# A hybrid attention and RWKV-7 block on one core: the recurrence cut into six parts a step for both directions side by side, and the first norm of the later tokens computed once and kept in DRAM

## The chip, the cores and the metric

The kernel runs on one core of one Trainium2 chip. TensorE (PE) does the matrix products, VectorE (DVE), ScalarE (ACT) and GpSimd (POOL) the element work, SyncE (SP) starts the transfers. The metric is the device time of one execution in microseconds (us).

## The reference, cut to what matters

One layer of a hybrid block over 2048 latent tokens and 256 context tokens, width 1024. What matters here is the first half of the layer, from the first norm to the merge of the two branches; the MLP behind it is the same in both kernels.

```python
h = modulate(rmsnorm(x, norm1_g), shift1, scale1)
hc = modulate(rmsnorm(xc, norm1_g), modc[0], modc[1])
q, k, v, rw, gl = jnp.split(h @ w_in, IN_SPLITS, axis=-1)
qc, kc, vc, rwc, glc = jnp.split(hc @ w_in, IN_SPLITS, axis=-1)
...
ya = latent_window_attention(q, k, v, kc, vc, sink)      # 16 blocks of 128 queries
...
for d, rev in enumerate((False, True)):                  # the recurrence, one scan a direction
    S_ctx, yc_d = wkv7_scan(S0, r_c, dec_c, kk_c, b_c, k_c, v_c, rev, update_ctx)
    _, y_d = wkv7_scan(S_ctx, r_l, dec_l, kk_l, b_l, k_l, v_l, rev, True)
    y_lat.append(y_d)
yr = rwkv_output(y_lat[0] + y_lat[1], r_l, v_l, hg_l, dirs_l, gate_g2, r_k, lnx_w, lnx_b)

x = x + gate1 * merge_branches(ya, yr, gl, w_branch_attn, w_branch_rwkv, w_out)
x = x + gate2 * sq_relu_mlp(modulate(rmsnorm(x, norm2_g), shift2, scale2), w_mlp_up, w_mlp_down)
```

## The kernel before, in words

The kernel has four stages. Each float32 product with weights is made of three matmuls on operands split in a high and a low part (`hh` and `hl` for the tokens, `w_hi` and `w_lo` for the weights).

**Stage 1** (0 to some 1060 us) is the first norm and the projection by `w_in`. The tokens are taken in three passes (`THIRDS`: 256 and 512, then 384 and 512, then 384 and 256 tokens), and each pass runs over 20 groups of weight columns. Ahead of each pass, `norm_block` loads the tokens of its two blocks, norms them (`x`, L180), transposes them on PE (`tr`, L186), scales (`hf`, L188, DVE) and splits them (`hh` on ACT, L192, `hl` on POOL, L193). `h_d` keeps `hf` for the first 1024 latent tokens, whose merge gates are computed later. Behind each pass `prepare` computes the inputs of the recurrence for those 256-token windows that are ready.

**Stage 2** (to 2540 us) is the recurrence with other work beside it. Per direction there are 36 steps of 64 tokens (`NCH`, `C`). For each window of four steps, `gram` makes small products (`g`, L517), and `inverse` inverts the 64x64 triangles on DVE: two long transposes of `ga` (`au`, L528), 31 small pairs of `itmp` (L534) and `tn` (L536), two long transposes into `st` (L545), and then two products on PE (`yp` L557, `zp` L569) with a third DVE transpose `t` (L549) ahead of them. This runs one window ahead. Each step of a direction has a `before` (its loads, `tb` and `gb`: L606 and L613) and a `chain`: products into one PSUM tile (`ch0` or `ch1`), a copy to `g` (L626, DVE), the product by `st` (L629), two copies into `w` (L630 ACT, L631 DVE), the next state (L636, L639, `w` L642) and the output (L650, L654). Beside every second step the function `beside` adds one whole attention block (`sc` scores, `mm` their minima, `sT` and `ops` the outputs), three columns of merge gates (`gt`, L215 to L217), and pieces of the second modulation (`adp`, L117 with `ada_w`); the last windows add four products of the attention branch (`branch`, `gt` L881 to L883, input `ya_h`, L873).

**Stage 3** (to 2900 us) is the merge, which begins with transposes of `yT` (`mt`, L990), and **stage 4** the MLP.

A scheduler orders the instructions of each engine when the kernel is built, by its own simulation of time; on the chip each engine then runs its list in that order. The pools of stage 2 get their memory when those of stage 1 are closed.

Of the kernel before, what the change touches and what calls it, by code (L numbers as in the profile page):

```python
# [47 lines left out]
def tile_hybrid_block(ctx: ExitStack, tc: tile.TileContext, io: dict, out: bass.AP):  # L48
# [8 lines left out]
    h_d = dram.tile([P, KC, GL8R], F32, name="h_d")  # L57
# [114 lines left out]
    def norm_block(t0, n, tag):  # L172
        hi = hpool.tile([P, KC, n], F32R, name=f"hh_{t0}", tag=f"hh{tag}")
        lo = hpool.tile([P, KC, n], F32R, name=f"hl_{t0}", tag=f"hl{tag}")
# [8 lines left out]
        for k in range(KC):  # L183
# [279 lines left out]
    def norms(blocks):  # L463
        return [norm_block(t0, n, "a" if i == 0 else "b") for i, (t0, n) in enumerate(blocks)]

    hs = norms(THIRDS[0])
    for i, wins in enumerate(ready):
        project(THIRDS[i], hs, groups[:20])
# [20 lines left out]
    atp = p2.enter_context(tc.tile_pool(name="atp", bufs=2, space=PSUM, reuse_waits="tile"))  # L489
    WS = 4  # L490
# [15 lines left out]
    def gram(ga, step, d):  # L506

        c = order[d][step]
        u0 = place(step, d)
        ka = rp.tile([P, NP, C], F32, name="kg")  # L510
        sp.dma_start(out=ka, in_=ka_d[d, c])
        bk = rp.tile([P, NP, P], F32, name="bkg")
        sp.dma_start(out=bk, in_=bk_d[d, c])
        g = bank(auxp, "g", "aux").rearrange("p (a b) -> p a b", b=C)
        for p in range(NP):
            for r in hh:
                pe.matmul(g[r, p], bk[r, p, 0:C], ka[r, p], start=True, stop=True)  # L517
        act.activation(ga[:, u0:u0 + NP], g[:, 0:NP], AF.Copy)

    def inverse(gl, sts):  # L520
# [10 lines left out]
        for k in range(31, 0, -1):  # L531
# [5 lines left out]
            if k % 6 == 0:  # L537
                yield
# [14 lines left out]
        for u0 in range(0, NU, HU):  # L553
            yp = bank(auxp, "yp", "aux").rearrange("p (u t) -> p u t", u=HU)
            for u in range(HU):
                for h in range(2):
                    pe.matmul(yp[h * C + 32:h * C + C, u], gl[h * C:h * C + 32, u0 + u, 32:64],  # L557
# [6 lines left out]
        for u0 in range(0, NU, HU):  # L564
            zp = bank(auxp, "zp", "aux").rearrange("p (u t) -> p u t", u=HU)
            for u in range(HU):
                for h in range(2):
                    r = slice(h * C + 32, h * C + C)
                    pe.matmul(zp[h * C:h * C + 32, u], ys[r, u0 + u], st[r, u0 + u, 32:64], start=True, stop=True,  # L569
# [9 lines left out]
    def open_step(step, d):  # L579
        s = Step()  # L580
        s.step, s.d, s.c, s.u = step, d, order[d][step], place(step, d)

        s.w = rp.tile([P, 2, 2, NP, C], F32, name="w", bufs=3)
        return s

    def before(s):

        d, c = s.d, s.c

        s.kr = rp.tile([P, 3, NP, C], F32, name="kr", bufs=3)  # L590
        bk = rp.tile([P, NP, 2, C], F32, name="bks")
# [11 lines left out]
        bk = bk.rearrange("p a b t -> p a (b t)")  # L603
        tb = bank(auxp, "tb", "aux").rearrange("p (a b) -> p a b", a=NP)
        for p in range(NP):
            pe.transpose(tb[:, p], bk[:, p], ident)  # L606
        s.bt = rp.tile([P, NP, P], F32, name="bt", bufs=3)
        act.activation(s.bt, tb, AF.Copy)
        s.bm = rp.tile([P, 2, NP, C], F32, name="bm", bufs=3)
        gs = [bank(auxp, "gb", "aux").rearrange("p (a j t) -> p a j t", j=2, a=NP) for h in range(2)]  # L610
        for p in range(NP):
            for h, r in enumerate(hh):
                pe.matmul(gs[h][:, p], bk[r, p], s.kr[r, h:3:2 - h, p], start=True, stop=True)  # L613
        for h in range(2):
            q = hh[1 - h]
            dve.tensor_tensor(out=s.kr[q, h], in0=gs[h][q, :, 0], in1=strict[q], op=ALU.mult)
            dve.tensor_tensor(out=s.bm[:, h], in0=gs[h][:, :, 1], in1=incl, op=ALU.mult)

    def chain(st, s, nxt):
        d, c, w = s.d, s.c, s.w  # L620
        cp = chp.tile([P, 2, NP, C], F32, name=f"ch{d}")
        for p in range(NP):
            for h, r in enumerate(hh):
                pe.matmul(cp[r, 0, p], s.kr[:, h, p], w[:, 1, h, p], start=True, stop=True)
        g = rp.tile([P, NP, C], F32, name="g")
        dve.tensor_copy(g, cp[:, 0])  # L626
        for p in range(NP):
            for r in hh:
                pe.matmul(cp[r, 0, p], st[r, s.u + p], g[r, p], start=True, stop=True)  # L629
        act.activation(w[0:C, 0, 0], cp[0:C, 0], AF.Copy)  # L630
        dve.tensor_copy(w[C:P, 0, 1], cp[C:P, 0])  # L631
        last = None
        if nxt is not None:

            for h, r in enumerate(hh):
                pe.matmul(cp[r, 0], ident[r, r], w[r, 1, h], start=True, stop=False, skip_group_check=True)  # L636
            for p in range(NP):
                for h, r in enumerate(hh):
                    last = pe.matmul(cp[r, 0, p], s.bt[:, p, r], w[:, 0, h, p], start=False, stop=True,  # L639
                                     skip_group_check=True)  # L640
            for h, r in enumerate(hh):
                dve.tensor_tensor(out=nxt.w[r, 1, h], in0=cp[r, 0],  # L642
                                  in1=pc[r, d, :, c:c + 1].broadcast_to([C, NP, C]), op=ALU.mult)
        if s.step < NCC:
            return
        yp = cp[:, 1]
        with tc.issue_after(last.ins) if last is not None else ExitStack():
            for p in range(NP):
                for h, r in enumerate(hh):
                    pe.matmul(yp[r, p], w[:, 0, h, p], s.bm[:, h, p], start=(p == 0), stop=False,  # L650
                              skip_group_check=True)
            for p in range(NP):
                for h, r in enumerate(hh):
                    pe.matmul(yp[r, p], w[r, 1, h, p], s.kr[r, 2, p], start=False, stop=True, skip_group_check=True)  # L654
        i = s.step - NCC
        lc = c - NCC
        src = yp if d == 0 else yp[:, :, ::-1]
        ysb = rp.tile([P, NP, C], F32, name="ysb")
# [671 lines left out]
```

## Time and profile before

| | us |
|---|---|
| median of 3 runs | 4351.41 |
| lowest and highest | 4349.32 and 4365.3 |
| profiled execution, its own time | 4355.38 |
| its span in the trace | 4353.6 |
| PE busy | 3976.6 (91%) |
| DVE, ACT, POOL busy | 2233.9, 1305.1, 1344.6 |

The span is the time from the first to the last instruction of the profiled execution; its own time lies 1.78 us above it, and 3.97 us above the median. The mean granted clock of PE was 0.929 of full speed. PE is busy nearly all the time, but its list also waits at certain places; the prediction reads the trace stage by stage for that.

### The profile page before, as it was taken

What the parts mean: (1) busy time and instruction counts of PE and PEld (TensorE: products, weight loads), DVE (VectorE), ACT (ScalarE), POOL (GpSimd) and SP (SyncE); (2) the same over time, 40 slices, a digit from 0 to 9 for tenths busy, and PEclk for the clock granted to TensorE, in tenths of its full rate; (3) what the DMA queues carried; (4) which work ended last, traced back from release to release, by engine and by line L of the source; (5) the groups of instructions that cost most, each with busy time, mean ns of one, the idle gap of its engine ahead of it and who ended that gap; (6) DMA issues with size and microseconds to landing.
All of it is one profiled execution on the core that took longest, in us unless ns stands there. A gap on an engine that the chain in (4) does not pass through costs nothing.

```text
span 4353.6 us, 67896 instructions
## 1 busy us (share of the span) xinstructions
PE 3976.6 (91%) x26788; PEld 3218.5 (74%) x26788; DVE 2233.9 (51%) x3918; ACT 1305.1 (30%) x2332; POOL 1344.6 (31%) x1120
## 2 busy tenths in 40 slices
PE   7989969894899999989989768998999999999999
PEld 5868868793677777767767646777888888888887
DVE  2264286687556646656674245434444436443434
ACT  3353444553322322223222213332222123212121
POOL 3353554542111111001000046523433233433332
PEclk8979989895999999889989779999999999999999
DMA  6555556665444543354453145452211113221111
GB/s 216 143 183 155 160 159 190 175 200 177 140 116 123 165 128 112 112 144 147 120 160 110 45 133 186 161 172 75 83 54 58 39 55 120 73 63 50 48 49 49
DMA packets 581874, 527.84 MB, mean 121 GB/s; under 512 B 118452, under 2 KB 492948, under 8 KB 580532
## 3 DMA queue, kind: packets, MB, share of 16 engines
q1 hardware_dynamic: 581556, 523.50, 39.9%
q8 instruction: 211, 3.46, 0.3%
q14 instruction: 107, 0.88, 0.1%
HBM read 383.19 MB, written 140.18 MB: 120 GB/s over the span
## 4 chain that ended last, share of the span: by engine, by line
PE 59%; DVE 9%; DMA 4%; issue 2%; POOL 2%; ACT 1%; SPq 1%; POOLq 0%; DVEq 0%; ACTq 0%
PE fd L1185 5%; PE fd L1184 5%; PE fd L1186 5%; PE fu L215 5%; PE fu L216 5%; PE fu L217 5%; PE gb L613 2%; PE ops L788 2%; DVE st L545 1%; PE sc L744 1%; DVE itmp L534 1%; PE mm L1099 1%; PE mm L1100 1%; PE mm L1101 1%; DVE tn L536 1%
## 5 line engine op out<-in xcount | busy, mean ns | idle before, releaser
L215 PE MATMUL acc<-hh,w_hi 128*128 128x384 f32 (+6 forms) x1304 | 460.1, 355 | 24.6 <-DVE st L227 8.7
L216 PE MATMUL acc<-hl,w_hi 128*128 128x384 f32 (+6 forms) x1304 | 461.2, 354 | 10.9 <-POOL hl L193 7.2
L217 PE MATMUL acc<-hh,w_lo 128*128 128x384 f32 (+6 forms) x1304 | 456.7, 352 | 10.2 <-POOL w_lo L209 8.9
L1190 DVE TENSOR_TENSOR acc<-fd,acc 128x512 f32<-128x512 f32 x480 | 322.2, 686 | 249.5 <-PE fd L1186 247.7
L1174 DVE TENSOR_TENSOR g_l<-rl,g_h 128x512 fp32r<-128x512 f32 x128 | 161.7, 1265 | 486.4 <-POOL rl L1173 486.4
L215 PE MATMUL fu<-h2h,up_h 128*128 128x512 f32 x1024 | 403.3, 394 | 5.1 <-ACT rl L1171 5.1
L1184 PE MATMUL fd<-dn_h,g_h 128*128 128x512 f32 x1024 | 399.7, 390 | 4.9 <-DVE acc L1188 4.9
L216 PE MATMUL fu<-h2l,up_h 128*128 128x512 f32 x1024 | 402.7, 393 | 0.0
L217 PE MATMUL fu<-h2h,up_l 128*128 128x512 f32 x1024 | 401.9, 393 | 0.0
L1185 PE MATMUL fd<-dn_l,g_h 128*128 128x512 f32 x1024 | 399.9, 391 | 0.0
L1186 PE MATMUL fd<-dn_h,g_l 128*128 128x512 f32 x1024 | 398.3, 390 | 0.0
L209 POOL TENSOR_TENSOR w_lo<-w_raw,w_hi 128x1024 fp32r<-128x1024 f32 (+1 forms) x92 | 223.2, 2428 | 229.9 <-ACT w_hi L208 213.4
L215 PEld LDWEIGHTS acc<-hh,w_hi 128*128 128x128 f32 (+2 forms) x1304 | 258.4, 199 | 48.2 <-DVE st L227 6.6
L1173 POOL TENSOR_TENSOR rl<-rl 128x512 f32<-128x512 f32 x128 | 146.3, 1144 | 474.8 <-ACT g_h L1172 474.7
L216 PEld LDWEIGHTS acc<-hl,w_hi 128*128 128x128 f32 (+2 forms) x1304 | 259.1, 199 | 34.4 <-POOL hl L193 11.5
L217 PEld LDWEIGHTS acc<-hh,w_lo 128*128 128x128 f32 (+2 forms) x1304 | 257.5, 198 | 33.5 <-POOL w_lo L209 11.1
L1171 ACT ACTIVATE rl<-fu 128x512 f32<-128x512 f32 x128 | 76.2, 597 | 661.5 <-PE fu L217 654.3
L1128 POOL TENSOR_TENSOR dn_l<-raw,dn_h 128x1024 fp32r<-128x1024 f32 x64 | 155.6, 2448 | 275.7 <-ACT dn_h L1127 275.7
L830 POOL TENSOR_TENSOR gw_lo<-gw_raw,gw_hi 128x1024 fp32r<-128x1024 f32 x32 | 76.7, 2398 | 519.2 <-ACT gw_hi L829 440.6
L215 PEld LDWEIGHTS fu<-h2h,up_h 128*128 128x128 f32 x1024 | 192.9, 188 | 48.7 <-ACT rl L1171 5.8
L1184 PEld LDWEIGHTS fd<-dn_h,g_h 128*128 128x128 f32 x1024 | 192.8, 188 | 46.0 <-DVE acc L1188 5.3
L217 PEld LDWEIGHTS fu<-h2h,up_l 128*128 128x128 f32 x1024 | 192.8, 188 | 43.2
(295 smaller groups left out, 8580.1 us busy)
## 6 DMA issues: line engine op xcount, KB each, us to landing
w_raw<-in_w_in SPq DMA_DIRECT2D x74, 512.0 KB
raw<-in_w_mlp_up SPq DMA_DIRECT2D x64, 512.0 KB
raw<-in_w_mlp_down SPq DMA_DIRECT2D x64, 512.0 KB
bk_d<-bk SPq DMA_DIRECT2D x36, 512.0 KB
bkg<-bk_d SPq DMA_DIRECT2D x72, 256.0 KB
w<-v_d SPq DMA_DIRECT2D x144, 128.0 KB
gw_raw<-in_w_in SPq DMA_DIRECT2D x32, 512.0 KB
ada_w<-in_w_ada SPq DMA_DIRECT2D x32, 512.0 KB
```

The source lines that it names most:

```text
L209: pool.tensor_tensor(out=lo[:, :, :m], in0=raw[:, :, :m], in1=hi[:, :, :m].bitcast(F32), op=ALU.subtract)
L215: pe.matmul(ps[:m, :n], wh[:, k, :m], hh[:, k, :], start=(k == 0), stop=False)
L216: pe.matmul(ps[:m, :n], wh[:, k, :m], hl[:, k, :], start=False, stop=False)
L217: pe.matmul(ps[:m, :n], wl[:, k, :m], hh[:, k, :], start=False, stop=(k == KC - 1))
L613: pe.matmul(gs[h][:, p], bk[r, p], s.kr[r, h:3:2 - h, p], start=True, stop=True)
L1128: eng.tensor_tensor(out=lo, in0=raw, in1=hi.bitcast(F32), op=ALU.subtract)
L1173: pool.tensor_tensor(out=rl, in0=rl, in1=rl, op=ALU.mult)
L1174: dve.tensor_tensor(out=glo[:, j], in0=rl, in1=gh[:, j].bitcast(F32), op=ALU.subtract)
L1184: pe.matmul(ps, lh, dn[j][0][:, cs], start=(j == 0), stop=False)
L1185: pe.matmul(ps, lh, dn[j][1][:, cs], start=False, stop=False)
L1186: pe.matmul(ps, ll, dn[j][0][:, cs], start=False, stop=(j == FG - 1))
L1190: dve.tensor_tensor(out=acc[:, cs], in0=ps, in1=acc[:, cs], op=ALU.add)
```

## The change

**The norms.** `norm_block` only yields `hf`. In the first pass, after each three of the first twelve weight groups, `norm_store` computes one of the four later blocks and stores its `hf` to `h_d`, which now covers all tokens. Ahead of passes two and three, `split_block` loads `hf` back through two buffers and splits it: the high part on ACT, the low part on POOL for odd `k` and on DVE for even `k`.

**The recurrence.** All matmuls of the recurrence go through `rpe`, which chains them in program order. `before` is cut in `load_step` (the loads, issued one step earlier), `turn` (the transposes `tb`) and `before` (`gb`). `chain` is cut in `chain_g`, `chain_u` and `chain_s`. A step has six parts: g, u and s for both directions, `turn` for both, and `before` for each. After each part the next window's work moves on by one yield (18 yields, the inverse yielding after three of its small pairs) and `beside` adds one iteration of attention, which interleaves the scores of a block with the outputs of the block before it, and one tick of filler: six matmuls of a gate (a quarter) or of a branch column (a half). The second modulation has one piece a step. The copies into `g` and the lower half of `w` move from DVE to ACT. `bkg` and `kg` are loaded one part earlier, `bkg` only in its used half; gate weights are loaded one gate earlier. The attention keys get a part for the context and two buffers of two blocks for the rest; `pT` has two buffers instead of three. The first window's inverse already has parts of step 0 and of `beside` between its yields.

```diff
-            if CTX <= t0 < CTX + GL8R:
-                sp.dma_start(out=h_d[:, k, t0 - CTX:t0 - CTX + n], in_=hf[:, :n])
-            act.activation(hi[:, k, :], hf[:, :n], AF.Copy)
-            pool.tensor_tensor(out=lo[:, k, :], in0=hf[:, :n], in1=hi[:, k, :].bitcast(F32), op=ALU.subtract)
+            yield k, hf[:, :n]
+
+    def norm_store(t0, n):
+        for k, hf in norm_block(t0, n):
+            sp.dma_start(out=h_d[:, k, t0:t0 + n], in_=hf)
+
+    def split_block(t0, n, tag):
...
+        def load():
+            for k in range(KC):
+                hf = epool.tile([P, 512], F32, name="hf")
+                sp.dma_start(out=hf[:, :n], in_=h_d[:, k, t0:t0 + n])
+                yield k, hf[:, :n]
+
+        first = (t0, n) in THIRDS[0]
+        for k, hf in norm_block(t0, n) if first else load():
+            if first and t0 >= CTX:
+                sp.dma_start(out=h_d[:, k, t0:t0 + n], in_=hf)
+            act.activation(hi[:, k, :], hf, AF.Copy)
+            (pool if first or k % 2 else dve).tensor_tensor(out=lo[:, k, :], in0=hf, in1=hi[:, k, :].bitcast(F32),
+                                                            op=ALU.subtract)
...
-        project(THIRDS[i], hs, groups[:20])
+        if i == 0:
+            for j, b in enumerate(b for third in THIRDS[1:] for b in third):
+                project(THIRDS[i], hs, groups[3 * j:3 * j + 3])
+                norm_store(*b)
+            project(THIRDS[i], hs, groups[12:20])
+        else:
+            project(THIRDS[i], hs, groups[:20])
...
+    class InOrder:
...
+        def link(self, r):
+            if self.last is not None:
+                tc.add_manual_dep(r.ins, self.last.name,
+                                  mybir.DependencyInfo(mybir.DependencyClass.NoSync, mybir.DependencyReason.DATA))
+            self.last = r.ins
+            return r
...
-        g = rp.tile([P, NP, C], F32, name="g")
-        dve.tensor_copy(g, cp[:, 0])
+                rpe.matmul(s.cp[r, 0, p], s.kr[:, h, p], w[:, 1, h, p], start=True, stop=True)
+        s.g = rp.tile([P, NP, C], F32, name="g", bufs=2)
+        act.activation(s.g, s.cp[:, 0], AF.Copy)
...
         act.activation(w[0:C, 0, 0], cp[0:C, 0], AF.Copy)
-        dve.tensor_copy(w[C:P, 0, 1], cp[C:P, 0])
...
+        act.activation(w[C:P, 0, 1], cp[C:P, 0], AF.Copy)
...
-            if step % 2:
-                beside(step // 2)
+            nxts = [open_step(step + 1, d) if step + 1 < NCH else None for d in range(2)]
+            for part in range(6):
+                if part == 0:
+                    for s in cur:
+                        chain_g(s)
+                    next(mods, None)
+                elif part == 1:
+                    for s in cur:
+                        chain_u(sts[w], s)
+                elif part == 2:
+                    chain_s(cur, nxts)
+                elif part == 3 and nxts[0] is not None:
+                    for s in nxts:
+                        turn(s)
+                elif part > 3 and nxts[0] is not None:
+                    before(nxts[part - 4])
+                next(ahead_of, None)
+                beside(TICKS)
+            cur = nxts
```

Three places of PE's list show how the change moves work. Behind the last product of the recurrence (`ch<-kr,w`), PE's list of before still has 84 score, 38 `sT` and 96 branch (`gt`) rows; these are its last four and the first of stage 3.

```order
L883 MATMUL gt<-ya_h,wa_l 128x512
L881 MATMUL gt<-ya_h,wa_h 128x512
L882 MATMUL gt<-ya_l,wa_h 128x512
L883 MATMUL gt<-ya_h,wa_l 128x512
L990 MATMUL mt<-ident,yT 128x128 x16
L1011 MATMUL mt<-ident,yc 128x128 x2
```

In the change, this is the end of the recurrence.

```order
L985 MATMUL gt<-ya_h,wa_l 128x512
L983 MATMUL gt<-ya_h,wa_h 128x512
L984 MATMUL gt<-ya_l,wa_h 128x512
L985 MATMUL gt<-ya_h,wa_l 128x512
L530 MATMUL ch_24128<-g,st 64x64 x8
L530 MATMUL ch_24117<-bm,w 64x64 x8
L530 MATMUL ch_24128<-bm,w 64x64 x8
L530 MATMUL ch_24117<-kr,w 64x64 x8
L530 MATMUL ch_24128<-kr,w 64x64 x8
L1142 MATMUL mt<-ident,yT 128x128 x16
L1163 MATMUL mt<-ident,yc 128x128 x2
```

The last branch column now lies between the u products and the output products of the last step, and stage 3 (`mt`) follows directly.

In the middle of stage 2, PE's list of before has here a gate column, then one direction's next state (`ident`, `bt`) without a row between its parts, and then the scores of one attention head.

```order
L217 MATMUL gt<-gh,gw_lo 128x512
L624 MATMUL ch_17824<-w,kr 64x64 x7
L636 MATMUL ch_17648<-w,ident 64x256 x2
L639 MATMUL ch_17648<-w,bt 64x64 x8
L624 MATMUL ch_17824<-w,kr 64x64
L613 MATMUL gb<-kr,bks 128x128 x8
L744 MATMUL sc_16355<-kA,qA 128x384
L746 MATMUL sc_16355<-kB,qB_9526 128x384
L744 MATMUL sc_16356<-kA,qA 128x256
L746 MATMUL sc_16356<-kB,qB_9526 128x256
```

In the change, a step's u products (`g,st`), the start of the next state of both directions (`w,ident`) and its sum (`w,bt`) have an output, a score and an `sT` piece between them.

```order
L530 MATMUL ch_15706<-g,st 64x64 x8
L530 MATMUL ch_15695<-w,ident 64x256 x2
L878 MATMUL ops<-vtok,pT 128x65 x4
L830 MATMUL sc_15937<-kAc,qA 128x256
L832 MATMUL sc_15937<-kBc,qB_9622 128x256
L868 MATMUL sT<-qA,kAc 128x512
L870 MATMUL sT<-qB_9621,kBc 128x512
L530 MATMUL ch_15706<-w,ident 64x256 x2
L530 MATMUL ch_15695<-w,bt 64x64 x8
L530 MATMUL ch_15706<-w,bt 64x64 x8
L830 MATMUL sc_15985<-kAl_9612,qA 128x384
```

What moved: the two directions stand side by side (two `ch` numbers), and each part is followed by pieces of attention that don't depend on it.

Ahead of the third pass of stage 1, PE's list of before has transposes of the tokens (`tr`) among the last products of the second pass (`acc`) and products of `prepare` (`zz_ps`).

```order
L186 MATMUL tr<-ident,x 128x128 x3
L216 MATMUL acc<-hl_4403,w_hi 128x384
L217 MATMUL acc<-hh_4402,w_lo 128x384
L413 MATMUL zz_ps<-xlr_4943,decay_w_r 128x256
L413 MATMUL zz_ps<-xlr_4949,iclr_a_r 128x256
L413 MATMUL zz_ps<-xlr_4943,decay_w_r 128x256
L413 MATMUL zz_ps<-xlr_4949,iclr_a_r 128x256
L215 MATMUL acc<-hh_4402,w_hi 128x384
L186 MATMUL tr<-ident,x 128x128 x3
L413 MATMUL zz_ps<-xlr_4943,decay_w_r 128x256
```

In the change there are none there; the transposes of all later tokens stand in the first pass, as here.

```order
L185 MATMUL tr<-ident,x 128x128 x3
L235 MATMUL acc<-hl_294,w_hi 128x512
L236 MATMUL acc<-hh_293,w_lo 128x512
L185 MATMUL tr<-ident,x 128x128 x3
L234 MATMUL acc<-hh_293,w_hi 128x512
L235 MATMUL acc<-hl_294,w_hi 128x512
```

What moved: 96 transposes and the DVE work around them, into a pass whose products need neither.

## Rows read from the trace of the kernel before

**Rows 1.** Stages: stretch, length, busy us by engine, PE clock, DMA share, GB/s

```profile
core 0: us, PE busy (x) PEld busy (x) DVE busy (x) ACT busy (x) POOL busy (x), PEclk, DMA share, GB/s
200.00:300.00 100.00, 81.04 (x327) 62.85 (x326) 69.45 (x120) 57.59 (x116) 63.98 (x73) 0.78 0.61 192
...
500.00:660.00 160.00, 120.62 (x594) 107.67 (x593) 112.36 (x202) 70.90 (x157) 88.09 (x89) 0.82 0.55 157
...
1000.00:1134.00 134.00, 65.75 (x583) 49.43 (x583) 92.67 (x183) 43.76 (x89) 37.00 (x50) 0.61 0.52 154
1134.00:2415.00 1281.00, 1205.51 (x13607) 927.06 (x13606) 765.91 (x1639) 350.43 (x631) 118.64 (x83) 0.94 0.45 132
2415.00:2540.00 125.00, 93.79 (x370) 69.99 (x370) 28.59 (x67) 21.33 (x35) 7.69 (x7) 0.70 0.19 62
2540.00:2660.00 120.00, 85.81 (x321) 59.76 (x322) 78.50 (x110) 36.68 (x53) 84.66 (x68) 0.77 0.52 154
```

**Rows 2.** Waits of PE in 500 to 660 us: total us, times, longest

```profile
PE tr L186 <- DVE x L180: 11.0, 1, 11.0
...
PE acc L216 <- POOL hl L193: 2.8, 4, 1.4
```

**Rows 3.** Waits of PE in 1000 to 1134 us

```profile
PE sc L744 <- DVE qA L729: 18.7, 1, 18.7
...
PE g L517 <- DMA bkg<-bk_d: 13.2, 3, 8.7
PE sc L744 <- DVE mm L754: 7.7, 5, 2.2
```

**Rows 4.** Waits of PE beside the recurrence, 1134 to 2415 us

```profile
PE sc L744 <- DVE mm L754: 10.8, 6, 3.7
PE adp L117 <- DMA ada_w<-in_w_ada: 10.6, 10, 1.7
PE yp L557 <- DVE t L549: 9.9, 6, 5.6
PE g L517 <- DMA bkg<-bk_d: 9.2, 5, 3.6
...
PE gb L613 <- DMA kr<-rho_d: 6.5, 5, 2.2
...
PE ch L629 <- DVE g L626: 3.9, 3, 2.2
```

**Rows 5.** Waits of PE behind the recurrence, 2415 to 2540 us

```profile
PE gt L881 <- ACT ya_h L873: 10.4, 2, 7.4
PE gt L881 <- DVE gt L884: 6.1, 7, 1.4
```

**Rows 6.** Groups by line and shape, 1134 to 2415 us: busy, mean ns, idle before

```profile
L545 DVE STREAM_TRANSPOSE st<-tn 32x1024 f32<-32x1024 f32 x32 | 63.1, 1972 | 0.8
...
L528 DVE STREAM_TRANSPOSE au<-ga 32x1024 f32<-32x1024 f32 x32 | 62.7, 1960 | 36.6 <-ACT ga L518 36.2
...
L626 DVE COPY g<-ch 128x256 f32<-128x256 f32 x72 | 30.0, 417 | 28.4 <-PE ch L624 27.4
L829 ACT ACTIVATE gw_hi<-gw_raw 128x1024 fp32r<-128x1024 f32 x28 | 29.6, 1056 | 75.4 <-PE gt L216 49.6 <-DMA gw_raw<-in_w_in 18.8 <-issue 6.9
```

**Rows 7.** Two neighbouring stretches of the recurrence, columns as in rows 1

```profile
1828.00:1862.00 34.00, 34.00 (x345) 25.77 (x345) 10.36 (x25) 6.81 (x14) 2.04 (x3) 0.50 0.15 44
1862.00:1896.00 34.00, 34.00 (x371) 26.96 (x371) 10.78 (x28) 11.75 (x22) 0.00 (x0) 1.00 0.24 67
```

**Rows 8.** Split of the norm's low part, 500 to 660 us, by line

```profile
L193 POOL TENSOR_TENSOR hl<-hf,hh 128x384 fp32r<-128x384 f32 x8 | 8.2, 1037 | 1.3 <-ACT hh L192 1.3
```

**Rows 9.** Timeline in the first window's inverse: start, us, engine, line

```profile
1075.02 0.42 DVE L534 TENSOR_TENSOR itmp<-tn,au 128x255 f32<-128x255 f32 x1
...
1077.65 3.20 POOL L840 TENSOR_TENSOR gl<-graw,gh 128x512 fp32r<-128x512 f32 x2 [22.23 <-ACT gh L839]
...
1078.34 1.38 DVE L534 TENSOR_TENSOR itmp<-tn,au 128x247 f32<-128x247 f32 x1
```

More of the change, by code (lines that the diff above doesn't have):

```diff
@@ L56, in tile_hybrid_block @@
     g_d = dram.tile([16, P, SEQ], F32, name="g_d")
-    h_d = dram.tile([P, KC, GL8R], F32, name="h_d")
+    h_d = dram.tile([P, KC, T], F32, name="h_d")
     ka_d = dram.tile([2, NCH, P, NP, C], F32, name="ka_d")
@@ L647, in chain @@
-        with tc.issue_after(last.ins) if last is not None else ExitStack():
+                    rpe.matmul(s.cp[r, 1, p], s.w[:, 0, h, p], s.bm[:, h, p], start=(p == 0), stop=False,
+                              skip_group_check=True)
+        for s in pair:
             for p in range(NP):
                 for h, r in enumerate(hh):
-                    pe.matmul(yp[r, p], w[:, 0, h, p], s.bm[:, h, p], start=(p == 0), stop=False,
+                    rpe.matmul(s.cp[r, 1, p], s.w[r, 1, h, p], s.kr[r, 2, p], start=False, stop=True,
@@ L651, in chain @@
                               skip_group_check=True)
[L652 to L658, printed above, removed]
-        if i < (NCH - NCC) // 2:
-            act.activation(ysb, src, AF.Copy)
-        else:
-            yo = rp.tile([P, NP, C], F32, name="yo", bufs=1)
-            sp.dma_start(out=yo, in_=y_d[lc])
-            dve.tensor_tensor(out=ysb, in0=src, in1=yo, op=ALU.add)
@@ L885, in branch @@
             sp.dma_start(out=ma_d[j, :, ts], in_=gt)
[L887 to L898 removed]
+            yield
+    load_k(kAc, kBc, 0, CTX)
@@ L925, in raw_of, with attend @@
-    def raw_of(shape):
-        return brp.tile(shape, F32, name="raw", tag="raw", bufs=2)
-    brp = wa = None
+    outs = 0
+    def attend():
+        nonlocal outs
+        prev = None
+        for n in range(NB + 1):
+            k = None
+            if n < NB:
+                k = Block()
+                k.n = n
+            a = scores(k) if k is not None else iter(())
+            b = outputs(prev) if prev is not None else iter(())
+            while True:
+                more = [next(b, b) is not b, next(a, a) is not a]
+                yield
+                more.append(next(b, b) is not b)
+                yield
+                if not any(more):
+                    break
+            outs = n
+            prev = k
@@ new lines, in fill, with raw_of @@
+    def fill():
+        work = [(t0, g) for t0 in range(0, GL8R, GBL) for g in range(16)]
+        nxt = load_gw(groups[20][2])
+        for i, (t0, g) in enumerate(work):
+            if g == 0:
+                h = load_h(t0)
+            w = nxt
+            if i + 1 < len(work):
+                nxt = load_gw(groups[20 + work[i + 1][1]][2])
+            yield from gate(g, *h, t0, w)
+        pg.close()
+        brp = p2.enter_context(tc.tile_pool(name="branch", bufs=1, reuse_waits="tile"))
+        def raw_of(shape):
+            return brp.tile(shape, F32, name="raw", tag="raw", bufs=2)
+        wa = branch_weights(brp, raw_of)
+        for t in range(SEQ // GBL):
+            while outs < (t + 1) * GBL // P:
+                yield
+            yield from branch(brp, raw_of, wa, t)
@@ new lines, in tile_hybrid_block, with beside @@
+    att, flr = attend(), fill()
+    TICKS = 1.0
+    credit = 0.0
+    def beside(ticks):
+        nonlocal credit
+        credit += ticks
+        if credit >= 1:
+            next(att, None)
+        next(flr, None)
+        if credit >= 1:
+            next(att, None)
+            credit -= 1
+    mods = (x for m in range(4) for x in ada2(m))
+    sts = []
+    cur = [open_step(0, d) for d in range(2)]
+    for s in cur:
+        for h, r in enumerate(hh):
+            pool.memset(s.w[r, 1, h], 0.0)
@@ L929, in tile_hybrid_block @@
+    for i, _ in enumerate(window(0, sts)):
+        if i == 4:
+            for s in cur:
+                turn(s)
+        if 5 <= i < 7:
+            before(cur[i - 5])
+        if i >= 4:
+            beside(1)
     for w in range(NWIN):
```

284 lines of the change are left out of this document (155 added, 129 removed).

## The prediction, as it was put on record

> **What bounds the kernel now.** I read first the table of stretches [rows 1], since the mean share of PE over the span hides where its time goes. For each stretch I work out what PE loses: its idle time (length less busy time) plus the busy time that a granted clock below full speed adds, taken as (1 - clock) x busy. That second part is an upper bound: small matmuls lose less at half clock, as the neighbouring stretches at 0.50 and 1.00 show, which got through 345 and 371 matmuls in the same 34 us [rows 7] (they are not the same matmuls, so this is a hint and no price). The losses are: 200 to 300 us, 19.0 + 17.8 = 36.8; 500 to 660 us (the change from the second to the third token pass), 39.4 + 21.7 = 61.1; 1000 to 1134 us (the lead-in of the recurrence), 68.3 + 25.6 = 93.9; the recurrence, 75.5 + 72.3 = 147.8; the stretch behind it, where only attention and one branch product are left, 31.2 + 28.1 = 59.3; the start of the merge, 34.2 + 19.8 = 54.0. The first five hold 399 us, and the change touches just these; the sixth and the MLP are not touched.
>
> Then I read PE's waits in each of them, to see what ended last. At the change of passes one wait for the normed tokens takes 11.0 us, and the low half of the split 2.8 [rows 2]. In the lead-in the list waits 18.7 us for the first queries, 13.2 for `bkg` and 7.7 for the minima of the scores [rows 3]. Beside the recurrence the waits are many and short: `mm` 10.8 us in 6 waits, `ada_w` 10.6 in 10, `yp` for a DVE transpose 9.9 in 6, `bkg` 9.2 in 5, `kr` 6.5 in 5, `g` 3.9 in 3 [rows 4]. Behind the recurrence the branch waits 10.4 us for `ya_h` and 6.1 for its own PSUM tile [rows 5]. So what bounds stage 2 is PE with a list that has nothing to put under a dependence at the wrong places; and PE has too little work at the two ends.
>
> **The change part by part.** *The work itself.* The 96 transposes of the later tokens move from the changes of passes into the first pass, at the same cost. The 32 new loads and 24 more stores of `h_d` are DMA work in stretches whose DMA share is 0.61 and 0.55 [rows 1]. The recurrence's products, the attention's and the gates' are the same in number. So the sum is one of lost time, stage by stage.
>
> *Token passes: -30 us.* The lines of the norm (load, `x`, `tr`, `hf`) leave the two stretches with 36.8 + 61.1 = 98 us lost. What else waits there is `prepare` and the weight splits, which stay. By the waits, 11.0 + 2.8 of the 39.4 us idle in the second stretch are the norm's [rows 2]; the clock that falls with these gaps and the DVE time that `prepare` gets back come on top. I take 30 of the 98. The best end is 60, if what is left waits no longer for a DVE that is 70% busy there. The worst end is 0: `hf` has two buffers for load and split, so a reloaded block comes at the pace of load and split, and PE may wait for that instead. The pace of the split alone: eight low parts of 1037 ns on POOL are 8.3 us a block [rows 8]; with every second one on DVE, 4.1 if the two engines run at once. They do not quite: while POOL splits gate tokens (two in 3.20 us), a DVE pair instruction of the inverse took 1.38 us in place of 0.42 [rows 9], so it stood still for most of a POOL instruction. One after the other, four on POOL (4.1 us) and four on DVE (0.42 us for 255 columns, so 0.63 each for 384, 2.5) are 6.6 us a block, still under the 8.3 of before; the sum has this in the 30.
>
> The Trainium skill, SBUF — State Buffer, section "Who interferes with whom", says that a DVE instruction with two SBUF inputs contends with a GpSimd instruction that reads SBUF and that one blocks until the other is done. By that rule the split on two engines is 6.6 us a block, and without it 4.1: over four blocks 10 us of the gain would go. The trace agrees, with 1.38 against 0.42 us [rows 9].
>
> In the first pass the added DVE work must fit: `hf`, `x` and the store of eight parts for each of four blocks. PE's list has 9 to 40 products between two groups of transposes there, so a late `hf` costs little; I put it at nothing and at 10 us if each of the four blocks makes PE wait 2.5 us, which lies in the range's low end.
>
> *Lead-in: -20 us.* The `bkg` load goes out one part earlier (13.2 us waited [rows 3]), and scores of one block, gates and step 0's `tb` and `gb` stand between the yields of the first inverse, so the waits for `mm` (7.7) get other work. The 18.7 us for the first queries stays: stage 2 gets its memory when stage 1 closes, and its first loads wait for that. Of 93.9 lost I take 20; ends 0 (the queue of first loads is longer now: gate weights, gate tokens, keys and queries together) and 45 (the waits for `bkg` and `mm`, 20.9, and the clock's 25.6 with them).
>
> *Beside the recurrence: -50 us.* Waits that the new order addresses: `ada_w` 10.6 (one piece a step, in another PSUM pool), `bkg` 9.2 and `kr` 6.5 (loads one part or one step earlier), `g` 3.9 (copy on ACT, with the other direction's products in between), `mm` 10.8 (a head's scores, then other work, then the next head), `yp` 9.9 in part. These are 51 of the 75.5 us idle; I take 35 of them, and 15 of the clock's 72.3 since gaps shrink. What is late next: DVE. The transposes for each window, 1.97 and 1.96 us each, four of each a window [rows 6], hold up what DVE does for the chain (`w`, `kr`), twice a window. And the gates end after 128 of the 216 ticks (32 columns of four), so that in the list about 12 of the 36 steps have neither a gate nor a branch product between their parts, and there only attention covers the copies. The best end is 100. The worst is a loss of 30: 12 steps that expose at each of three parts two copies of 417 ns [rows 6], one after the other on one engine.
>
> *Behind the recurrence: -50 us.* PE's list has nothing there but the merge. The 96 branch products and two attention blocks of the end (93.8 us busy) now stand under the last steps as cover, at the same PE time, so what goes is the lost 59.3, less what they lose under the last steps. I take 50, ends 35 and 59. The merge's start waits for its own loads as before and keeps its 54.0; with the tail gone, nothing of it can be fetched under it, which is inside the 35.
>
> *Sum.* 30 + 20 + 50 + 50 = 150 us of the profiled execution's 4355.4 (span 4353.6 and 1.8 around it): 4205. The median of the runs lies 4.0 us below that execution, so 4201; I say **4200**. The worst ends together give 5 us, the best 264.
>
> **The rivals.** *Small gain, about 4280.* The waits beside the recurrence only change their names: an in-order list with DVE's transposes ahead of it stalls where the scheduler could go around. Then only the tail and part of the ends come, 50 + 20: 4280. For it: DVE is busy 766 of 1281 us there [rows 1], and no term makes that less but the copies of 417 ns, 72 of them [rows 6], 30 us, and as many to `w`. Against it: the ready work (attention, gates) is placed behind each part.
>
> *Slower, above 4373.* Each of the 216 parts must end before the next can begin, on copies that now stand in ACT's queue behind `gw_hi` (1056 ns [rows 6]) or an exponential. The place is `g` and `u` of each step. The price: if a part waits 1 us beyond what its pieces cover, 216 us come on the forecast, 4201 + 216 = 4417. It decides at (4373 - 4201) / 216 = 0.80 us a part. Against it: in two thirds of the steps each part is followed by six 512-column products as well as an attention piece, and the copy is 417 ns. The clock would go with it: the stretch at 0.50 had no idle time at all, only many small matmuls [rows 7], so contiguous small ones may bring it on.
>
> *Larger gain, about 4110.* The recurrence loses only some 50 us, and the token passes 40: 60 + 40 + 90 + 55 = 245, 4106.
>
> *The norms bring nothing.* The reload through two buffers takes what the transposes gave: 4230, inside the range.
>
> **How the numbers follow.** Forecast, including the norms that bring nothing (gain of 80 to 230): 0.62. Small gain (22 to 80): 0.15. Larger: 0.09. No change, within 0.5% (22 us, about what a measurement of this kernel can tell from nothing): 0.05. Slower: 0.09. So faster 0.86, same 0.05, slower 0.09. The range leaves out the slower and unchanged cases and about half of the larger gain: 4085 to 4300.
>
> **What would show it.** Right: no PE work of attention or branch behind the last `ch` product, and `mt` within some 10 us of it; the waits for `ada_w`, `bkg`, `kr` gone; PE idle beside the recurrence under 45 us; no `tr` of tokens after some 250 us. Wrong: PE waits for copies on ACT (`g`, `w`) or for `hf` reloaded at the start of the passes by tens of us; a granted clock beside the recurrence well under 0.94; or more PE time per step than before, which would mean that the pieces delay the chain and not that they cover it.

## The result, and the profile after

The changed kernel takes **4233.95 us** (median; 4228.55 to 4238.27) against 4357.48 for the kernel before, run on the same chip: ratio 0.9716, 95% interval 0.9691 to 0.9741. The forecast was 4200 in a range of 4085 to 4300. The profiled execution has a span of 4234.0 us, 119.6 shorter than that of before. All ratios here are to the kernel before on the chip of the same run; one slow execution of 11754.33 us, in the run with attention issued earlier, is left out of its ratio.

Where the 119.6 us came from, by the start of the first or last instruction of a kind on PE in both traces:

| | before | after | length before | length after |
|---|---|---|---|---|
| last product of the projection (`acc`) | 996.9 | 977.3 | 996.9 | 977.3 |
| first chain product (`ch`) | 1134.3 | 1116.3 | 137.4 | 139.0 |
| last chain product | 2412.9 | 2416.6 | 1278.6 | 1300.3 |
| first transpose of the merge (`mt<-yT`) | 2542.9 | 2425.2 | 130.0 | 8.6 |
| first MLP product (`fu`) | 2902.8 | 2783.1 | 359.9 | 357.9 |
| last MLP product (`fd`) | 4343.7 | 4223.8 | 1440.9 | 1440.7 |

The stretch behind the recurrence is gone (-121.4), stage 1 gave 19.6, the lead-in nothing, and the recurrence grew by 21.7, with the work of the old stretch inside it. A second trace of the changed kernel, with a span of 4212.7 us, has its first and last chain product at 1112.4 and 2396.2: there the recurrence is 1283.8 us long and grew by 5.2 only. So some 15 us between two single traces are no finding by themselves.

The table of stretches of the changed kernel answers to [rows 1]: second pass to third, lead-in, recurrence, what lies behind it, start of the merge.

```profile
core 0: us, PE busy (x) PEld busy (x) DVE busy (x) ACT busy (x) POOL busy (x), PEclk, DMA share, GB/s
...
500.00:640.00 140.00, 105.18 (x483) 90.80 (x483) 97.78 (x171) 61.89 (x137) 70.46 (x69) 0.80 0.58 168
...
980.00:1116.00 136.00, 79.86 (x647) 60.79 (x648) 102.27 (x203) 47.44 (x93) 42.36 (x49) 0.65 0.55 157
1116.00:2417.00 1301.00, 1169.45 (x13931) 908.66 (x13924) 724.69 (x1549) 421.02 (x806) 121.67 (x87) 0.92 0.45 128
2417.00:2425.00 8.00, 0.00 (x0) 0.00 (x0) 0.42 (x1) 1.26 (x2) 2.52 (x2) 0.75 0.65 191
2425.00:2543.00 118.00, 87.95 (x321) 59.21 (x322) 77.97 (x110) 36.78 (x53) 86.16 (x68) 0.76 0.53 157
```

The recurrence has 1301.0 - 1169.5 = 131.5 us without PE work, against 75.5 before. PE's waits there answer to [rows 4].

```profile
PE ch L530 <- DVE kr L671: 15.8, 4, 7.4
PE gb L530 <- issue: 11.5, 4, 7.4
PE sT L868 <- DVE mm L840: 11.4, 9, 3.9
PE sc L830 <- DVE mm L840: 10.8, 9, 3.5
...
PE ch L530 <- ACT w L690: 7.2, 5, 4.9
PE gb L530 <- DVE bm L673: 6.8, 2, 6.5
...
PE g L530 <- DMA bkg<-bk_d: 3.7, 5, 1.5
```

`ada_w` and the DMA wait for `kr` have left the top of the list, and `bkg` fell from 9.2 to 3.7. In their place PE waits for DVE: `kr` (15.8), `bm` (6.8), `mm` (22.2 in two rows), and 11.5 at `gb` with no releaser named. The timeline of DVE around one such wait, and PE's behind it:

```profile
2076.26 7.66 DVE L577 STREAM_TRANSPOSE au<-ga 32x1024 f32<-32x1024 f32 x4 [0.35 <-ACT ga L567]
...
2085.46 0.43 DVE L671 TENSOR_TENSOR kr<-gb,cc 64x256 f32<-64x256 f32 x1
2085.92 0.42 DVE L673 TENSOR_TENSOR bm<-gb,cc 128x256 f32<-128x256 f32 x1
```

```profile
2077.86 0.69 PE L530 MATMUL ch<-w,kr 128*64 128x64 f32 x16
2085.94 0.48 PE L530 MATMUL ch<-w,kr 128*64 128x64 f32 x2 [7.40 <-DVE kr L671]
```

The four transposes stand in one row of 7.66 us, and the masked copies of the step (`kr`, `bm`) come behind them and behind two instructions on `qB`; PE's next product in the list needs `kr`, and all products behind it in the list wait too, for 7.40 us.

In the token passes and the lead-in, the waits that answer to [rows 2, 3] are these (first fence 500 to 660 us, second 980 to 1116):

```profile
PE bon_ps L475 <- DVE ks L472: 15.3, 4, 5.9
PE acc L234 <- ACT hh L210: 12.5, 4, 9.7
```

```profile
PE g L530 <- DMA bkg<-bk_d: 15.1, 3, 11.4
PE sc L830 <- ACT kAl L782: 11.8, 1, 11.8
PE sc L830 <- DVE mm L840: 8.5, 6, 3.9
```

The 11.0 us for the normed tokens are gone, and 12.5 for reloaded high parts (`hh`) have come; `bkg` is waited for 15.1 us in the lead-in, against 13.2 before.

### The profile page after: what moved, and what is told of

Same layout as the page of the kernel before. It is cut to its first block, busy times and chain, and to the rows that moved or that the text cites. A ratio compares the mean times of both kernels' runs of the same rounds, so it can differ in the third digit from the quotient of the medians.

```text
span 4234.0 us, 67809 instructions
## 1 busy us (share of the span) xinstructions
PE 3851.0 (91%) x26788; PEld 3128.3 (74%) x26788; DVE 2185.5 (52%) x3794; ACT 1358.0 (32%) x2476; POOL 1340.7 (32%) x1104
## 4 chain that ended last, share of the span: by engine, by line
PE 56%; DVE 10%; DMA 4%; issue 2%; POOL 2%; ACT 1%; SPq 1%; POOLq 0%; DVEq 0%; ACTq 0%
PE fd L1336 5%; PE fd L1337 5%; PE fd L1338 5%; PE fu L234 5%; PE fu L235 5%; PE fu L236 5%; PE ch L530 4%; PE gt L942 3%; PE ops L878 3%; DVE au L577 2%; PE gb L530 2%; DVE tn L585 1%; DVE st L594 1%; DVE itmp L583 1%; PE sc L830 1%
## 5 line engine op out<-in xcount | busy, mean ns | idle before, releaser
L234 PE MATMUL acc<-hh,w_hi 128*128 128x384 f32 (+6 forms) x1304 | 457.9, 353 | 37.7 <-ACT hh L210 17.6
L235 PEld LDWEIGHTS fu<-h2l,up_h 128*128 128x128 f32 x1024 | 193.1, 189 | 42.8
```

The lines of the kernel that those rows point to most:

```text
L234: pe.matmul(ps[:m, :n], wh[:, k, :m], hh[:, k, :], start=(k == 0), stop=False)
L235: pe.matmul(ps[:m, :n], wh[:, k, :m], hl[:, k, :], start=False, stop=False)
```

## The experiments

**The norms alone and the recurrence alone.** The first has stage 1 of the change and the recurrence of before, the second the reverse.

```diff
--- the norms alone: the kernel before with
+            for j, b in enumerate(b for third in THIRDS[1:] for b in third):
+                project(THIRDS[i], hs, groups[3 * j:3 * j + 3])
+                norm_store(*b)
--- the recurrence alone: the changed kernel with
-                project(THIRDS[i], hs, groups[3 * j:3 * j + 3])
-                norm_store(*b)
...
+        project(THIRDS[i], hs, groups[:20])
```

> The kernel before with only the change of the norms (the first norm of the later tokens in the first pass, kept in DRAM, reloaded and split); the recurrence as before. Theory: the terms add up, so this is worth the 17 to 20 us by which stage 1 ended earlier in the changed kernel: ratio to before 0.9955 (0.993 to 0.997), with PE waiting for the reloaded high parts (hh) for 10 to 20 us. Rival: what stage 1 gives is taken back in the lead-in of the recurrence, which waits for the last prepared window and for its own first loads: within 5 us of before.

> The changed kernel with stage 1 as before (each block normed ahead of its own pass); recurrence and what runs beside it as changed. Theory: 99 to 108 us of the gain are stage 2's, ratio 0.976 (0.973 to 0.979), and nearly all of it is the work behind the last chain product, which goes under the last steps. Rival: stage 2 depends on what stage 1 leaves (DVE and queues free earlier), then less than 85 us.

The norms alone: ratio 0.9999 (0.9976 to 1.0021), 4349.02 us. In their trace stage 1 ends at 972.9 us, 24.0 earlier than before and more than the 17 to 20 expected, and PE waits 16.8 us for `hh`, as expected. But within the interval the time gains 0.24% (10 us) at the most: the ratio fits the rival. The rival's mechanism isn't shown: the lead-in grew by 4.8 us only (142.2 against 137.4), so the first chain product still comes 19.1 us earlier. Where the gain goes stays open. The recurrence alone: 4256.02 us, 0.9792 (0.9753 to 0.9831); the ratio is beyond my bounds by a little. The changed kernel and the recurrence alone were then measured on one chip.

> The changed kernel once more, on the chip of the three below, so that they are compared on one chip. Ratio to before 0.9716 as measured first, 0.969 to 0.974.

> The changed kernel with stage 1 as before, beside the changed kernel on one chip. The norms alone on the old recurrence gave 0.9999 (0.9976 to 1.0021), and their lack under the new one a ratio of 0.9792 against 0.9716. Theory: the norms are worth the 15 to 20 us that their profile shows in both cases: 10 to 22 us slower than the changed kernel here. Rival: they are worth nothing by themselves: within 6 us.

On one chip the changed kernel takes 4230.48 us (0.9691, 0.966 to 0.9722) and the recurrence alone 4249.32 (0.9745, 0.9711 to 0.9778). Under the new recurrence the norms are worth 18.8 us by the medians; the intervals just overlap, but the slowest of six executions of the changed kernel (4236.8) is faster than the fastest of six without the norms (4245.9). So stage 2's part is 96 us in the first measurement and 115 of 134 in the second. That the norms give less under the old recurrence is likely by the first run, not settled.

**The reload's buffers.**

```diff
-                hf = epool.tile([P, 512], F32, name="hf")
+                if k % 2 == 0:
+                    x = xpool.tile([P, D], F32, name="x")
+                hf = x[:, k % 2 * 512:k % 2 * 512 + n]
```

> The changed kernel, but the reloaded hf goes through the four token buffers that are free then (room for eight parts) in place of two buffers. Theory: the start of passes two and three is paced by two buffers and a landing of 2.5 us, so PE's wait for hh (17.6 us in the first 1000 us) falls below 5 and stage 1 ends 8 to 20 us earlier. Rival: the pace is that of the split on ACT, DVE and POOL or of SP's queue, and prepare takes the rest: stage 1 ends within 4 us of the changed kernel's.

4218.24 us, ratio 0.9697 (0.9663 to 0.973). The waits in its first 1000 us:

```profile
PE acc L237 <- POOL hl L213: 4.1, 2, 3.1
...
PE acc L236 <- ACT hh L212: 1.5, 1, 1.5
```

`hh` falls from 17.6 to 1.5 us, and stage 1 ends at 932.0 us in place of 977.3, more than the bounds. But the first chain product comes at 1096.8, 19.5 us earlier only: the lead-in grew from 139.0 to 164.8 us. So two buffers paced the passes, and the lead-in takes back more than half of what stage 1 gives. By the medians the kernel gains some 16 us; the ratio's interval holds the changed kernel's 0.9716, so that gain isn't shown by this run alone.

**The split of the low part.**

```diff
-            (pool if first or k % 2 else dve).tensor_tensor(out=lo[:, k, :], in0=hf, ...
+            pool.tensor_tensor(out=lo[:, k, :], in0=hf, ...
```

> The changed kernel with the low halves of the reloaded tokens all on POOL. Theory: POOL and DVE block each other when both read two operands, and the reload is paced by its loads anyway, so the split on two engines is worth nothing: within 8 us of the changed kernel, PE's wait for hh about the same. Rival: the split paces the reload and POOL alone makes stage 1 10 us or more longer.

4241.97 us (0.9721, 0.9692 to 0.9751) against 4230.48 on the same chip; the intervals overlap. PE's wait for `hh` is 17.7 us against 17.0, and stage 1 ends at 976.2 against 973.3. So the split doesn't pace the reload, as the buffers already said. The 11 us of the medians are more than the theory's 8, and all six executions lie above all six of the changed kernel (4237.36 at the least, 4236.8 at the most there); 2.9 us of them are in stage 1, and where the others come from stays open.

**DVE's transposes spread.**

```diff
             dve.transpose(out=au[r], in_=gl[r, :, o:o + 32].rearrange("p u t -> p t u"))
-        yield
+            yield
...
-            if k % 3 == 0:
+            if k % 4 == 0:
                 yield
...
             dve.transpose(out=st[r, :, o:o + 32].rearrange("p u t -> p t u"), in_=tn[r])
+            if qd < 3:
+                yield
```

> The changed kernel, but the four long DVE transposes at the head and at the end of a window's inverse are one yield apart each in place of four in a row (7.65 us), and the small pairs yield after every fourth. Theory: DVE's block of 7.65 us is what PE's waits for kr (15.8 us), bm (6.8) and the unnamed ones at gb (11.5) come from; they fall below 12 us together and the time by 15 to 35 us against the changed kernel. Rival: PE's list is fixed, so the waits only move to the other users of DVE (mm, qA, w): within 8 us of the changed kernel.

4223.4 us, 0.9707 (0.9678 to 0.9737). Its waits beside the recurrence:

```profile
PE sT L870 <- DVE mm L842: 18.4, 8, 3.9
PE gt L985 <- DVE gt L988: 16.9, 6, 4.5
PE sc L832 <- DVE mm L842: 10.8, 6, 4.3
...
PE ch L530 <- DVE kr L673: 8.4, 5, 4.1
...
PE gb L530 <- issue: 5.7, 3, 2.8
...
PE gb L530 <- DVE bm L675: 1.7, 3, 0.8
```

`kr` is 8.4 with a longest of 4.1 (7.4 in the change), `gb` 5.7 and `bm` 1.7: of 34.1 us 18.3 went, and the three are 15.8 together, not below 12. But `mm` rose from 22.2 to 29.2 and `gt` from 9.3 to 16.9. So DVE's block was a cause of these waits, as I said, and under a fixed list part of them moved to DVE's other users, as the rival has it. The time is 10.6 us lower by the medians of two chips, between the bounds of theory and rival (15 and 8); the interval holds the changed kernel's 0.9716, so a gain isn't shown.

**The copies back on DVE.**

```diff
-        act.activation(s.g, s.cp[:, 0], AF.Copy)
+        dve.tensor_copy(s.g, s.cp[:, 0])
-        act.activation(w[C:P, 0, 1], cp[C:P, 0], AF.Copy)
+        dve.tensor_copy(w[C:P, 0, 1], cp[C:P, 0])
```

> The changed kernel with the copies into g and the lower half of w back on DVE. Theory: the move to ACT took them out from behind DVE's transposes and small pairs; back on DVE, PE waits for g and w for 15 to 30 us more beside the recurrence, and the time is 10 to 30 us longer than the changed kernel's 4234. Rival: ACT's queue (gate weights 1.06 us, exponentials 0.6) holds them as long: within 8 us.

4254.28 us, 0.9757 (0.9732 to 0.9783). Of its waits beside the recurrence:

```profile
PE sT L868 <- DVE mm L840: 22.7, 9, 7.8
...
PE ch L530 <- DVE w L690: 12.8, 12, 4.9
...
PE ch L530 <- DVE g L682: 4.0, 3, 3.3
```

PE waits 12.8 us for the copy into `w` (L690), where it waited 7.2 for it on ACT, and 4.0 for `g` (L682): 9.6 us more, less than the theory's 15 to 30. At `sT` it waits 22.7 us for `mm` in place of 11.4. By the medians the time is 20.3 us longer, within the theory; by the ratios moving the copies to ACT is worth some 18 us (0.0041 of the time). The two intervals overlap at their ends (0.9732 and 0.9741), so the gain is likely and its size open.

**No tie between the recurrence's products.**

```diff
-    rpe = InOrder()
+    rpe = nc.tensor
```

> The changed kernel with the recurrence's matmuls not tied to program order; only the six parts and the pieces between them. In PE's list 36 branch rows now stand behind the last chain product, against none. Theory: the fine pieces bring the gain and the tie is only a safeguard: within 20 us of the changed kernel, of which about 10 are the 36 rows behind the recurrence. Rival: the tie is what keeps the attention in step with the recurrence: 40 us or more of the gain go.

4207.86 us, 0.9652 (0.9631 to 0.9674): 26 us faster than the changed kernel by the medians, with an interval wholly below that of the changed kernel's first measurement (0.9691 to 0.9741) and overlapping that of its second (0.966 to 0.9722). The theory's 20 us were passed, on the side of a gain where it had priced a loss; the rival is out. Without the tie the first chain product is issued at 1041.3 us, before the first inverse is done, so the recurrence has no comparable start. From the last product of the projection to the merge, with the columns of [rows 1], for the kernel before, the change and this run:

```profile
996.90:2542.90 1546.00, 1365.69 (x14565) 1047.03 (x14563) 887.34 (x1888) 415.91 (x756) 165.50 (x140) 0.89 0.44 128
```

```profile
977.30:2425.20 1447.90, 1250.49 (x14573) 970.34 (x14571) 830.09 (x1760) 472.11 (x907) 166.55 (x138) 0.89 0.46 131
```

```profile
975.80:2388.60 1412.80, 1284.40 (x14514) 999.34 (x14572) 822.92 (x1760) 471.63 (x907) 165.35 (x138) 0.92 0.47 135
```

The first waits beside the recurrence without the tie (1105 to 2365 us):

```profile
PE ops L878 <- ACT pT L875: 12.7, 6, 8.1
PE ch L680 <- DVE kr L671: 8.2, 8, 2.2
PE sT L868 <- DVE mm L840: 6.5, 6, 2.4
```

PE is idle for 180.3 us before, 197.4 in the change and 128.4 without the tie, and `kr` is waited for 8.2 us in 8 short waits, the longest 2.2 in place of 7.4: the list has other products ahead. The pieces alone empty the stretch behind the recurrence (17.1 us from the last chain product to the merge, with 36 branch rows). The tie has a use too: PE is busy 33.9 us less with it, for which the next section has a cause. But it costs 69.0 us of idle time.

**The kernel before, with attention and branches issued earlier.**

```diff
-        while seen < min(NB, w + 1):
+        while seen < min(NB, w + 3):
-        while w >= 12 and done < (1, 1, 2, 3, 3, 4)[w - 12]:
+        while w >= 12 and done < (1, 2, 3, 4, 4, 4)[w - 12]:
```

> The kernel before with only this: each attention block is issued in the code two calls (four steps) earlier, and the branch products two calls earlier. Theory: the place in the code doesn't move the tail, since whole blocks are coarse and the scheduler puts them where its own simulation has PE free; PE's list still has 294 rows behind the last chain product (288 before): within 15 us of before, and 100 us or more between the last chain product and the merge. Rival: an earlier place is enough: 30 to 60 us faster than before, and the stretch behind the recurrence under 60 us.

4375.7 us, 1.0035 (1.0014 to 1.0056), and 137.4 us between the last chain product (2416.6) and the merge (2554.0). So this other place in the code doesn't move the stretch. What is left, with the tie and the place ruled out, is the cut into pieces with something to add behind each part; it was not tried by itself.

**The amendments together.** The first has the spread transposes and the reload's buffers, the second the reload's buffers and no tie.

> The changed kernel with both amendments: the transposes one yield apart, and the reload through the four token buffers. Theory: they lie in different stages and add up, 10 and 16 us: 4200 to 4215, ratio to before 0.966 to 0.969. Rival: what the one gives the other takes in the lead-in: no better than 4218.

> The changed kernel without the tie between the recurrence's matmuls, and with the reload through the four token buffers. Theory: the two gains (26 us and 16 us) lie in different stages; stage 1 ends some 45 us earlier and the lead-in takes half of that back: 4180 to 4200 where the changed kernel has 4234, ratio to before 0.960 to 0.963. Rival: without the tie the lead-in is already short, so nothing of the second is taken back: under 4175; or the scheduler uses the earlier start to put attention ahead of the chain: no better than 4205.

4202.33 us (0.964, 0.9617 to 0.9663) for the first, and **4182.5 us** (0.9589, 0.9558 to 0.962) for the second, the latter on the chip where the changed kernel takes 4230.48. Both times are in the theory's ranges, and both ratios a little below them. The second is the fastest of all, 4.1% under the kernel before. Its trace doesn't show where the gain over the run without the tie lies: in that execution, the slowest of its six (4196.7), stage 1 ends 43.2 us earlier (932.6 against 975.8), but the merge begins only 2.0 us earlier (2386.6 against 2388.6).

## Why the prediction was right, point by point

The direction and the size held: a gain of 123.5 us by the medians where 150 was forecast. The way there did not hold in all parts, and that the two largest terms came out in sum is luck, as shown below. Of the signs of being right, the empty stretch behind the last chain product came, the waits for `ada_w` and the DMA wait for `kr` went, `bkg` fell to 3.7 us beside the recurrence, and the last transpose of tokens is at 190.5 us. PE's idle time beside the recurrence, forecast under 45 us, did not come. Of the signs of being wrong, a wait for `hh` of 17.6 us came.

- *Behind the recurrence, -50, together with beside the recurrence, -50.* From the first chain product to the merge, 1408.6 us became 1308.9: -99.7, as the sum of the two had it. The main reason is right: no product of attention or branch stands behind the last chain product, and the merge follows 8.6 us later. The other place in the code doesn't do this (1.0035), and the tie isn't needed for it (0.9652); the cut into pieces is what is left.
- *How the recurrence gets there* was wrong. I had PE's idle time there fall to under 45 us; it rose from 75.5 to 131.5. The 15 us for the clock did not come either: by the prediction's own measure, (1 - clock) x busy, the recurrence lost 72.3 us before and about 93.6 after, at a granted clock of 0.92. What I took as fixed, the PE time of the same products, fell instead: from the last product of the projection to the merge PE is busy for 1365.7 us before and 1250.5 after, 115 us less for the same products, by a profile that models where a product ends. Of these, 81 us are gained without the tie as well (1284.4). The products `gb`, which read the upper or the lower half of the partitions, show one cause; the groups of before, of the change and of the run without the tie (busy us, mean ns), each with 1152 records:

```profile
L613 PE MATMUL gb<-kr,bks 64*128 64x128 f32 x1152 | 143.6, 297 | 6.5 <-DMA kr<-rho_d 6.5
```

```profile
L530 PE MATMUL gb<-kr,bks 64*128 64x128 f32 x1152 | 113.2, 310 | 19.9 <-issue 11.5 <-DVE bm L673 6.8 <-ACT bt L660 1.1
```

```profile
L668 PE MATMUL gb<-kr,bks 64*128 64x128 f32 x1152 | 141.2, 302 | 2.5 <-issue 2.3 <-DVE bm L673 0.2
```

The mean of one hardly changes (297 to 310), but the busy time is 143.6, 113.2 and 141.2. The code writes these products with the two halves in turn, and the tie keeps that order. In PE's lists, where one `gb` product follows another, it is on the other half in all 477 cases in the change, in 197 of 441 before and in 190 of 449 without the tie. The starts in the traces fit: 453, 216 and 270 of the 1152 records begin within 20 ns of the record ahead. So records of different halves begin almost together; no run changed this order by itself. One step's rows in the timeline of before and of the change:

```profile
1513.18 0.93 PE L613 MATMUL gb<-kr,bks 64*128 64x128 f32 x10
...
1514.95 0.71 PE L613 MATMUL gb<-kr,bks 64*128 64x128 f32 x6
```

```profile
1535.62 1.16 PE L530 MATMUL gb<-kr,bks 64*128 64x128 f32 x16
```

Sixteen records take 1.16 us in one row, and 0.93 + 0.71 = 1.64 us in two. In the one row they begin in pairs, 6 or 7 ns apart within a pair and most pairs 105 ns after the last; in the two rows four of them begin alone, 105 to 112 ns after the one ahead, and the change to another kind of product comes twice, with 201 ns from the start of the last record to the next product each time. From the last product of the projection to the merge, PE changes from one kind of product to another 3383 times before, 2959 times in the change and 3178 times without the tie. At 201 - 105, or some 0.1 us each, the change's 424 fewer are 42 us; this is an estimate from these rows at full clock. `gb` gives 30 of the 115 us, which includes its own share of the row changes; how the rest divides stays open.

So the step that failed is "the sum is one of lost time" at fixed work, with the waits beside the recurrence: a saving of PE time that I had not seen and new waits cancelled, some of them behind DVE's transposes, which I had named as next but priced too low. The rival "small gain", in which an in-order list stalls where the scheduler could go around, was right in its mechanism: with the tie PE is idle 69.0 us longer, and the kernel takes 26 us more on balance.

- *Token passes, -30.* The term was too large: 19.6 us in the traces, 18.8 by the medians under the new recurrence, and nothing that could be measured under the old one. The worst end that I had named came half true: the reload through two buffers paces the passes (17.6 us for `hh`, 1.5 with more buffers). The estimate by the pace of the split (6.6 us a block) looked at the wrong pace; it is the load's. The trace of the change still shows DVE held up beside POOL, as in [rows 9]: a low part on DVE took 412 ns at the least and 2378 at the most, and the longest stands beside a split of weights on POOL:

```profile
587.35 2.71 POOL L228 TENSOR_TENSOR w_lo<-w_raw,w_hi 128x1024 fp32r<-128x1024 f32 x1 [6.84 <-ACT w_hi L227]
```

```profile
588.10 2.38 DVE L211 TENSOR_TENSOR hl<-hf,hh 128x384 fp32r<-128x384 f32 x1 [0.25 <-ACT hh L210]
```

- *Lead-in, -20.* It gave nothing: 137.4 us became 139.0, with 14 us more PE work in it (79.9 us busy against 65.8). The end that I had put at 0, a longer queue of first loads, is what the traces show. Before, the first `bkg` load is issued at 998.5 us, 1.6 us behind the last product of the projection; in the change it comes at 998.4, 21.1 us behind it, and the loads of step 0 (`bks`, `kr`, `w`) now stand ahead of it in SP's list. The first rows of the window's small products (`g`) and the loads, before and after:

```profile
998.49 0.44 SPq L513 DMA_DIRECT2D bkg<-bk_d  x1
```

```profile
1003.03 1.12 PE L517 MATMUL g<-kg,bkg 64*64 64x64 f32 x16
```

```profile
979.74 0.51 SPq L643 DMA_DIRECT2D bks<-bk_d  x1
...
993.45 3.98 SPq L650 DMA_DIRECT2D w<-v_d  x1
997.46 0.88 SPq L555 DMA_DIRECT2D kg<-ka_d  x1
998.39 0.57 SPq L557 DMA_DIRECT2D bkg<-bk_d  x1
```

```profile
1007.44 1.97 PE L530 MATMUL g<-kg,bkg 64*64 64x64 f32 x32 [11.44 <-DMA bkg<-bk_d]
```

From the last product of the projection to the first `g` it takes 6.1 us before and 30.1 in the change, 6.5 with the norms alone and 28.5 with the recurrence alone, so the delay comes with the new recurrence. The last `g` of the first window starts 41.0 us behind the projection before and 52.6 in the change, 11.6 later; from it to the first chain product it takes 86.4 us in place of 96.4. So 10.0 us are gained there, half of what was forecast, and 11.6 are lost ahead of it. That the order of the loads is the cause is read from the traces; no run changed it. With the reload's buffers stage 1 ended 45 us earlier and the first chain product came 19.5 earlier; what holds the lead-in there was not taken apart.
- *Copies on ACT* were part of the recurrence's term; alone they are worth some 18 us by the ratios, with intervals that overlap. The slower rival, which made them a loss, is out.

## What to carry to other kernels

Work that can run beside a serial chain helped here in pieces small enough to stand between the chain's parts: whole blocks stayed behind the chain at both places in the code that were tried, and pieces of six products didn't. A hand-made order over an engine's list should be tried with and without its tie: here the pieces brought the gain, and the tie lost part of it again where one operand came late. When a reload replaces a computation, count the buffers that hold the landing, and look at whether the next stage can start earlier at all, and at which loads stand first in its queue.

## What the runs showed of the hardware

The busy time of PE for the same products depends on their order: 16 records of `gb` in one row took 1.16 us, and in two rows of 10 and 6 took 1.64. Records of the two halves of the partitions that stand in turn begin 6 or 7 ns apart; those that stand alone begin 105 to 112 ns after the one ahead. Over the kernel this is 30 us for `gb` alone (143.6 against 113.2), with hardly a change in the mean of one. So PE's 91% before and 91% after stand for 3976.6 and 3851.0 us on the same 26788 records.
